# Two decoder layers on one core: pair-wide operations, f32 roots as split pairs, layer 1's low weight parts made ahead, and a searched order

## The chip, the cores and the metric

The kernel runs on one core of a Trainium2 chip. The time is device microseconds of one execution of the whole program; the median of several executions is compared. PE is the matmul engine, PEld its weight loads, DVE, ACT and POOL the vector, scalar and general engines, and SP the engine whose queue issues nearly all DMA transfers.

## The reference

Two layers over 1024 tokens of width 1024, all in float32. Each layer has one input projection feeding four mixers, a norm of each mixer's output, one output projection, and a gated FFN:

```python
for l in range(DEPTH):
    proj = rmsnorm(x, attn_norm[l]) @ w_in[l]
    (c_q, c_kv, k_r, g_b, g_c, u_conv, u_pool, q_sw, k_sw, v_sw) = jnp.split(proj, pts, axis=-1)
    y_a = mla_attention(c_q, c_kv, k_r, mla_q_norm[l], mla_kv_norm[l], w_uq[l], w_ukv[l], cos, sin)
    y_b = short_gated_conv(g_b, g_c, u_conv, conv_w[l])
    y_c = multiscale_pool(u_pool, pool_w[l], pool_scale[l])
    y_d = swa_sink_attention(q_sw, k_sw, v_sw, swa_sinks[l], slopes)
    gf = jnp.stack([y_a, y_b, y_c, y_d], axis=2)
    gf = gf * lax.rsqrt(jnp.mean(gf * gf, axis=-1, keepdims=True) + RMS_EPS)
    x = x + (gf.reshape(b, s, D_MIX) * mix_norm[l]) @ w_o[l]
    gate, up = jnp.split(rmsnorm(x, ffn_norm[l]) @ w_gate_up[l], 2, axis=-1)
    x = x + (jax.nn.silu(gate) * up) @ w_down[l]
return rmsnorm(x, final_norm)
```

`y_d` is attention in a window of 128 tokens with two key heads for four query heads; a sink logit per head is added to the softmax's denominator. The widths are 256 per mixer, 2816 in the FFN.

## The kernel before

**Precision.** Every operand of a matmul is held as two fp32r parts: a high part (an ACT cast, L342 or L216) and a low part (a DVE subtraction of the high part from the f32 value, L345 or L217). `split` does this for one tile, with an optional gain per row (L347 on ACT, L348 on DVE). `mm3` (L322) makes three matmuls of each term: high by high, high by low, low by high. The activations are transposed: 128 channels in the partitions, tokens along the row, in two halves of 512 tokens (`t` = 0, 1). SBUF is cut into 47 slots of 128 x 1024, each a pair of halves; `F.half`, `F.pair`, `R.half` and `R.pair` take them as f32 or fp32r.

**Stages of a layer.** (1) The mixers: 15 blocks of `w_in` (128 output channels each; 48 matmuls per block for both halves) with their consumers, then the latent attention with the output projection's blocks for groups b, c, d woven in, then the rest of the output projection. (2) The gate and up products, as a fast 2x2 algorithm with seven products instead of eight; `combine` (four calls) makes its sums of activations, `hb[N1]`, `hb[N2]`, `hb[T3]`, `hb[T4]`, out of half tiles. (3) The down projection with the same algorithm: 28 units (`units`, seven products by four blocks) of 33 matmuls each. Its weights come by `dn_raw` two units ahead and are split one unit ahead; its activations come back from DRAM (`ad`) by `dn_acts`.

**Weights.** `weights` loads a block as f32 (up to 512 KB), casts it on ACT and subtracts on DVE, into one of two ring places. `expect_layer` lists a layer's 15 `w_in` blocks and 8 `w_o` blocks in the order of use (the first three `w_in` blocks of layer 0 are loaded apart), `ahead` fetches the next one.

**Keys and queries of the window attention.** The key tile `pk` is scaled to f32 per half (L421). For each key head its 64 rows are cast and subtracted into their own rows of two tiles and again into the other 64 rows (L604 to L607), since a query tile holds its high part in one half of the rows and its low part in the other (`swa_q`, L529 to L534). `swa_unit` makes one block of 128 tokens for a key head: scores (L638), a biased minimum on DVE (L648), the exponent on ACT with its sum (L661), and the sink's exponent (DVE L671, ACT L672), which is added to the sum (L673).

**Roots.** `SumSq` adds up squares (ACT L377/L386, DVE L388/L394). `rnorm` sums over the partitions with a matmul by a matrix of ones and takes the inverse root by Ln, Exp and one correction (L411 to L417). If the object was made with `pair`, the sum is split into high and low first, and two fp32r matmuls with `ones_r` follow (L402); otherwise one f32 matmul with `ones` does it (L405), which the trace records as two. The entry norm, groups c and d and the query rank use L405.

**The order.** All instructions are traced once, and the class `Order` makes a list schedule from modelled costs: an order for each engine, a PSUM bank for each tile and a slot for each tile by its modelled end. `scheduled_kernel` repeats tracing and planning four times, keeps the plan with the shortest modelled span, and imposes its order on every engine's queue (SP's among them).

Of the kernel before, what the change touches and what calls it, by code (L numbers as in the profile page):

```python
# [13 lines left out]
F32 = mybir.dt.float32  # L14
# [5 lines left out]
P = 128  # L20
# [17 lines left out]
N_U = 47  # L38

# [83 lines left out]
def trunk_kernel(ctx: ExitStack, tc: tile.TileContext, ins, out, given=None, ends=None):  # L123
# [80 lines left out]
    def weights(src, n):  # L204
        if n > 2 * P:
            s = F.pair()
            raw = F.ap2(s)
            sp.dma_start(raw[:, :n], src)
            hi, lo = (R.ap2(i) for i in ring_next())
            F.free_pair(s)  # L210
        else:
            raw = wpool.tile([P, 2 * P], F32, name="vraw", tag="vraw")
            sp.dma_start(raw[:, :n], src)
            hi = wpool.tile([P, 2 * P], F32R, name="vhi", tag="vhi")
            lo = wpool.tile([P, 2 * P], F32R, name="vlo", tag="vlo")
        act.copy(hi[:, :n], raw[:, :n])  # L216
        dve.tensor_tensor(out=lo[:, :n], in0=raw[:, :n], in1=rd(hi[:, :n]), op=ALU.subtract)  # L217
        return hi, lo
# [16 lines left out]
    def expect(f, *args):  # L235
        stream.append((f, args))

    def expect_layer(l):
        for m in (2, 3, 0, 4, 5, 6, 1, 13, 14, 10, 11, 12, None, 7, 8, 9):
            if m is None:  # L240
                expect(rope_weights, l)
            else:
                if l or m not in (2, 3, 0):
                    expect(weights, ins["w_in"][l, m], 2 * HT)
        for d in range(NK):
            expect(weights, ins["w_o"][l, d, :, 2 * P :], 6 * P)
# [113 lines left out]
    class SumSq:  # L360
# [9 lines left out]
        def add(self, t, f, cols=whole, after=None):  # L370
            e = EPS * self.n / P
            m = self.done[t, cols.start] = self.done.get((t, cols.start), 0) + 1
            if self.acc[t] is None:
                self.acc[t] = F.half()
            a = F.ap(self.acc[t])[:, cols]
            if m == 1:
                sq = act.activation(a, f, AF.Square)  # L377
                if after is not None:
                    behind(sq, after)
                if self.n == P:  # L380
                    dve.tensor_scalar(out=a, in0=a, scalar1=e, scalar2=None, op0=ALU.add)
# [4 lines left out]
            act.activation(q, f, AF.Square)  # L386
            if m == self.n // P - self.held.get((t, cols.start), 0):
                dve.scalar_tensor_tensor(  # L388
                    out=a, in0=q, scalar=e, in1=a, op0=ALU.add, op1=ALU.add
                )  # L390
# [89 lines left out]
    for l in range(L):  # L480
# [34 lines left out]
        def ytiles(g):  # L515
            y[g] = [[F.half() for _ in range(2)] for _ in range(2)]
# [4 lines left out]
        def swa_q(m, pp):  # L521
            for t in range(2):
                f = tmp()
                dve.scalar_tensor_tensor(
                    out=f, in0=pp[t], scalar=0.125, in1=r_of(t), op0=ALU.mult, op1=ALU.mult
                )
                e, o = R.half(), R.half()
                qs[2 * m][t], qs[2 * m + 1][t] = e, o
                act.copy(R.ap(e)[hd], f[hd])  # L529
                act.copy(R.ap(o)[tl], f[tl])  # L530
                dve.tensor_tensor(
                    out=R.ap(e)[tl], in0=f[hd], in1=rd(R.ap(e)[hd]), op=ALU.subtract
                )
                dve.tensor_tensor(  # L534
                    out=R.ap(o)[hd], in0=f[tl], in1=rd(R.ap(o)[tl]), op=ALU.subtract
                )
# [61 lines left out]
        kk = [[R.pair(), R.pair()] for _ in range(2)]  # L598
        for t in range(2):
            f = tmp()  # L600
            mul_to(f, pk[t], r_of(t))
            for g, own, oth in ((0, hd, tl), (1, tl, hd)):
                k1, k2 = R.ap(kk[g][0] + t), R.ap(kk[g][1] + t)
                act.copy(k1[own], f[own])  # L604
                act.copy(k1[oth], f[own])
                dve.tensor_tensor(out=k2[own], in0=f[own], in1=rd(k1[own]), op=ALU.subtract)
                dve.tensor_tensor(out=k2[oth], in0=f[own], in1=rd(k1[own]), op=ALU.subtract)  # L607
# [19 lines left out]
        def swa_unit(g, i):  # L627
# [42 lines left out]
            sk = par[:, l * PC_N + PC_SINK + 2 * g : l * PC_N + PC_SINK + 2 * g + 2]  # L670
            dve.tensor_tensor(out=es, in0=nm, in1=sk, op=ALU.add)  # L671
            act.activation(es, es, AF.Exp)  # L672
# [79 lines left out]
        def group_split(g, t):  # L752
            for c in range(2):
                s = y[g][c][t]
                mixed[g, c, t] = half_split(F.ap(s), pcol(l, PC_MIX + 2 * "abcd".index(g) + c))
                F.free(s)
# [51 lines left out]
        for ct in range(2):  # L808
# [37 lines left out]
            F.free_pair(b)  # L846
            for t in range(2):
                h, lo = half_split(dst[:, t * HT : (t + 1) * HT])
# [10 lines left out]
        for t in HALVES:  # L859
            group_split("c", t)  # L860
# [7 lines left out]
        sq_q = SumSq(2 * P)  # L868
        for m in range(2):
            pp = project() if m else nextp  # L870
            for t in range(2):
                f = tmp()
                mul_to(f, pp[t], r_of(t))
                cq[m][t] = half_split(f, pcol(l, PC_QN + m))
                sq_q.add(t, f)
            swa_some(2)
# [306 lines left out]
        def combine(j):  # L1183
# [7 lines left out]
            n1, n2, t3, t4 = tmp("tp"), tmp("tp"), tmp("tp"), tmp("tp")  # L1191
# [7 lines left out]
            hb[T3][j] = half_split(t3)  # L1199
# [8 lines left out]
            hb[T4][j] = half_split(t4)  # L1208
# [27 lines left out]

        def pair_split(s, after=None):
            h, lo = R.pair(), R.pair()
            split(R.ap2(h), R.ap2(lo), F.ap2(s), after=after)
            return h, lo  # L1240
# [146 lines left out]
        for t in HALVES:  # L1387
            group_split("d", t)
# [3 lines left out]
        for n, (h, t) in enumerate(steps):  # L1392
# [8 lines left out]
            if n == 0:  # L1401
# [10 lines left out]
                group_split("b", 1)  # L1412
                group_split("b", 0)
# [369 lines left out]
        tail = []  # L1783
        for n, (c, m) in enumerate(units):
            if n + 2 < len(units):
                raws.append(dn_raw(*units[n + 2]))
# [67 lines left out]
class Order:  # L1854
# [10 lines left out]
    def __init__(self, traced, edges, banks=True):  # L1865
# [114 lines left out]
    def run(self, rank, back=False):  # L1980
# [5 lines left out]
        late, cost, kind = self.LATE[back], self.cost, self.kind  # L1986
        left = [len(w) for w in wait]
# [16 lines left out]
        for _ in range(self.n):  # L2004
            best = None
            for e in self.ENGINES:
                due(e, free[e])
                if not now[e] and not later[e]:
                    continue
                t = free[e] if now[e] else later[e][0][0]  # L2010
# [5 lines left out]
            due(e, t)  # L2016
            k = heapq.heappop(now[e])[1]
            seen, taken = cost[k]
            order[e].append(k)
# [17 lines left out]
            for j, sync in ahead[k]:  # L2037
# [9 lines left out]
                if not left[j]:  # L2047
                    heapq.heappush(later[self.engine[j]], (ready[j], j))
        return end, order

    def find(self, passes=3):
# [6 lines left out]
        return best  # L2058

# [38 lines left out]
def scheduled_kernel(fresh, ins_of, rounds=4):  # L2098
# [18 lines left out]
    plan = Order(traced, nc.dependency_edges)  # L2117
    end, best = plan.find()[2], None
    for _ in range(rounds):
        given = plan.banks(end), plan.ends(end, asked)  # L2120
        nc, traced, asked = trace(*given)
        plan = Order(traced, nc.dependency_edges)
        span, order, end = plan.find()
        if best is None or span < best[0]:
            best = span, given, order
# [134 lines left out]
```

## Time and profile before

| what | us |
|---|---|
| median of 3 runs | 2050.09 (2048.81 to 2051.84) |
| the profiled execution | 2051.07 |
| its span, first to last instruction | 2049.3 |
| PE busy | 2029.5 |
| DVE busy | 1521.4 |
| ACT busy | 988.8 |
| POOL busy | 568.7 |

Times in the trace count from the span's start. A group's row in a list by shape shows line, engine, operation, output from input, shapes and count, then busy us and the mean ns of one, then the engine's idle time before these instructions with what ended it. A timeline's row shows start us, length us and count of merged instructions; matmuls overlap in a pipeline and their ends are modelled, so the length of a merged row is the start of its last matmul plus one whole duration. A DMA row gives count, KB each and median us from issue to landing.

### The profile page before, as it was taken

To read this page: it belongs to the slowest core of one execution; us is meant where nothing else is said; L and a number is where in the kernel's file an instruction comes from. 1 tells how busy PE (TensorE), PEld (TensorE's weight loads), DVE (VectorE), ACT (ScalarE), POOL (GpSimd) and SP (SyncE) were. 2 spreads that over 40 slices of the span, in tenths; PEclk is the share of its full clock that TensorE was granted. 3 is DMA by queue.
4 is the path that set the end of the run, shared out by engine and by line. 5 is a ranking of instruction groups with operands and counts; after the bars stand their busy time and mean duration, and the time that the engine had idled before them with its cause. 6 is when DMAs were issued, how large, how long until landed. Compare 5 with 4: busy or idle time off the path is not lost.

```text
span 2049.3 us, 26536 instructions
## 1 busy us (share of the span) xinstructions
PE 2029.5 (99%) x9422; PEld 1675.6 (82%) x9422; DVE 1521.4 (74%) x2443; ACT 988.8 (48%) x1737; POOL 568.7 (28%) x428
## 2 busy tenths in 40 slices
PE   9999999999999999999999999999999999999998
PEld 7887888878888888888888878888788888888887
DVE  8779978997666768655657898889966666685555
ACT  7447657753333335434433666667433333354342
POOL 0100000047786772000001000000577777710000
PEclk9999999999999999999999999999999999999999
DMA  5431232334555556766424213232455555487552
GB/s 203 97 76 41 74 104 79 141 134 154 199 174 187 180 167 250 269 217 197 157 59 94 52 52 102 74 108 110 150 176 187 176 175 176 162 298 258 178 188 87
DMA packets 144294, 305.51 MB, mean 149 GB/s; under 512 B 13985, under 2 KB 61089, under 8 KB 144161
## 3 DMA queue, kind: packets, MB, share of 16 engines
q1 hardware_dynamic: 139680, 292.27, 41.8%
q0 software_dynamic: 4480, 11.54, 3.2%
q8 instruction: 74, 1.21, 0.2%
q14 instruction: 60, 0.48, 0.1%
HBM read 219.34 MB, written 94.90 MB: 153 GB/s over the span
## 4 chain that ended last, share of the span: by engine, by line
PE 91%; DVE 5%; issue 1%; DMA 1%; ACT 1%; POOL 0%; SPq 0%; DVEq 0%; ACTq 0%; POOLq 0%
PE ps_mm L322 35%; PE ps_s L322 28%; PE ps_t L322 10%; PE ps_pv L322 8%; PE ps_pv L1090 2%; PE ps_t L1078 1%; DVE u L345 1%; PE ps_s L1024 1%; PE ps_s L1026 1%; PE ps_s L1025 1%; DMA u<-in_w_gu 1%; PE ps_s L896 1%; DVE u L348 1%; PE ps_pv L699 1%; PE ps_s L638 1%
## 5 line engine op out<-in xcount | busy, mean ns | idle before, releaser
L322 PE MATMUL ps_mm<-u,u 128*128 128x512 f32 (+1 forms) x3378 | 833.3, 390 | 4.4 <-ACT u L342 1.5
L322 PEld LDWEIGHTS ps_mm<-u,u 128*128 128x128 f32 x3378 | 615.0, 188 | 131.3 <-issue 5.5
L322 PE MATMUL ps_s<-u,u 128*128 128x512 f32 x2670 | 634.4, 390 | 2.8 <-DVE u L345 1.7
L345 DVE TENSOR_TENSOR u<-u,u 128x1024 fp32r<-128x1024 f32 (+2 forms) x400 | 453.3, 1152 | 231.6 <-ACT u L342 161.1
L322 PEld LDWEIGHTS ps_s<-u,u 128*128 128x128 f32 x2670 | 500.4, 188 | 110.8 <-DVE u L345 4.0
L342 ACT CAST u<-u 128x1024 fp32r<-128x1024 f32 (+2 forms) x400 | 345.8, 882 | 456.2 <-PE ps_mm L322 72.1
L322 PE MATMUL ps_t<-u,u 128*128 128x512 f32 (+1 forms) x1124 | 254.2, 378 | 1.1 <-DVE u L1309 1.1
L322 PEld LDWEIGHTS ps_t<-u,u 128*128 128x128 f32 x1124 | 202.1, 188 | 41.7 <-DVE u L1309 1.6
L1502 POOL TENSOR_TENSOR tp<-tp,u 128x512 f32<-128x512 f32 x80 | 126.3, 1579 | 345.0 <-ACT tp L1500 345.0
L322 PE MATMUL ps_pv<-u,u 128*128 128x512 f32 x744 | 177.1, 389 | 0.0
L322 PEld LDWEIGHTS ps_pv<-u,u 128*128 128x128 f32 x744 | 139.6, 188 | 29.1
L296 POOL DMA_DIRECT2D gd<-in_w_gu x24 | 22.1, 921 | 421.5 <-PE ps_t L322 283.9
L1087 POOL MEMSET u<- 128x128 f32 x32 | 6.1, 221 | 431.3 <-PE ps_pv L1090 148.8
L1500 ACT ACTIVATE tp<-tp 128x512 f32<-128x512 f32 x80 | 50.6, 632 | 147.9 <-DVE tp L421 147.8
L347 ACT ACTIVATE u<-u,par 128x512 fp32r<-128x512 f32 x100 | 70.4, 717 | 37.4 <-DVE u L421 11.0
L342 ACT CAST u<-ps_t 128x512 fp32r<-128x512 f32 (+3 forms) x132 | 65.1, 503 | 47.9 <-PE ps_t L1078 26.7
L348 DVE SCALAR_TENSOR_TENSOR u<-u,par,u 128x512 fp32r<-128x512 f32 x100 | 73.3, 745 | 17.6 <-ACT u L347 17.4
L345 DVE TENSOR_TENSOR u<-ps_t,u 128x512 fp32r<-128x512 f32 (+3 forms) x132 | 75.4, 580 | 12.7 <-ACT u L342 10.9
L1580 POOL TENSOR_TENSOR u<-u,u 128x352 f32<-128x352 f32 x64 | 82.7, 1293 | 2.9 <-DMA u<-in_w_dn 1.5
L1580 POOL TENSOR_TENSOR u<-u 128x352 f32<-128x352 f32 x64 | 82.1, 1284 | 4.6 <-DMA u<-in_w_dn 3.9
L386 ACT ACTIVATE tn<-u 128x512 f32<-128x512 f32 (+1 forms) x91 | 52.9, 596 | 57.2 <-DVE u L1771 47.9
L1290 POOL TENSOR_TENSOR u<-u 128x512 f32<-128x512 f32 x38 | 69.5, 1829 | 21.8 <-DVE u L345 21.8
(203 smaller groups left out, 2347.4 us busy)
## 6 DMA issues: line engine op xcount, KB each, us to landing
u<-in_w_gu SPq DMA_DIRECT2D x84, 512.0 KB, 4.2
ad<-u SPq DMA_DIRECT2D x154, 256.0 KB, 2.4
u<-ad SPq DMA_DIRECT2D x70, 512.0 KB, 4.7
u<-in_w_dn SPq DMA_DIRECT2D x64, 352.0 KB, 3.6
qd<-u SPq DMA_DIRECT2D x64, 352.0 KB, 2.6
u<-qd SPq DMA_DIRECT2D x32, 512.0 KB, 5.0
u<-in_w_in SPq DMA_DIRECT2D x28, 512.0 KB, 3.5
u<-in_w_dn SPq DMA_DIRECT2D x24, 512.0 KB, 5.2
```

Of the source, the lines that this page charges most:

```text
L296: paced(pool.dma_start(d, a, **more))
L322: last_mm = pe.matmul(o, w, r, start=start and k == 0 and i == 0, stop=stop and k == n - 1 and i == 2, skip_group_check=again,)
L342: a = act.copy(hi, f)
L345: dve.tensor_tensor(out=lo, in0=f, in1=rd(hi), op=ALU.subtract)
L347: a = act.activation(hi, f, AF.Copy, scale=gain)
L348: dve.scalar_tensor_tensor(out=lo, in0=f, scalar=gain, in1=rd(hi), op0=ALU.mult, op1=ALU.subtract)
L386: act.activation(q, f, AF.Square)
L1090: pe.matmul(py[:, c0:], v_of(j, h), R.ap(s)[:, c0:], start=j == 0 and n == 0, stop=j == nj - 1 and n == 1,)
L1290: pool.tensor_tensor(out=q4, in0=q4, in1=F.ap(self.raw[1] + 1), op=ALU.add)
L1500: last_silu = act.activation(g, g, AF.Silu)
L1502: pool.tensor_tensor(out=g, in0=g, in1=r, op=ALU.mult)
L1580: pool.tensor_tensor(out=o, in0=a, in1=b, op=ALU.add)
```

## The change

Six edits, all in one step:

- **Low parts made ahead.** In layer 0's down projection (units 2 to 27), `prepare` loads each of layer 1's 23 weight blocks, splits it, and stores the low part to DRAM. In layer 1 `weights` loads raw values and the stored low part, and only casts the high part.
- **Roots.** `SumSq.add_pair` adds squares over both halves at once and, if `pair` is set, splits the sum. Groups c and d and the query rank are set to `pair`; the entry norm is not.
- **Halves joined.** Window queries and keys, `group_scale`, `group_split`, the pool's output, the query rank's split and the splits in `combine` work on 1024 columns where they worked on two tiles of 512.
- **Key copies.** The key tiles' other 64 rows are filled by four SP transfers a layer (256 KB each) instead of casts and subtractions.
- **Sink.** The sink's exponent takes the sink as its bias: two ACT instructions of one column a unit instead of a DVE addition and an ACT instruction of two columns.
- **Planner.** It plans twice (costs of DVE and ACT as modelled, and 3% longer), one round each instead of four. Each plan is improved by 30 random changes of the ranks where PE waits, kept if the modelled span doesn't grow; the order taken is the one with the smallest mean over six trials with random delays.

```diff
+SLOW = (1.0, 1.03)
+PREP = (1, 27)
...
+    def prepare(key, src, n):
+        s, h, lo = F.pair(), R.pair(), R.pair()
+        raw = F.ap2(s)[:, :n]
+        sp.dma_start(raw, src)
+        split(R.ap2(h)[:, :n], R.ap2(lo)[:, :n], raw)
+        F.free_pair(s)
+        R.free_pair(h)
+        prepared[key] = dpool.tile([P, n], F32, name="ph%s%d_%d" % key)
+        sp.dma_start(prepared[key], rd(R.ap2(lo)[:, :n]))
+        R.free_pair(lo)
+
-    def weights(src, n):
+    def weights(src, n, key=None):
...
+            if key in prepared:
+                sp.dma_start(rd(lo[:, :n]), prepared[key])
+                act.copy(hi[:, :n], raw[:, :n])
+                return hi, lo
...
+    def pair_split(s, gain=None, after=None):
+        h, lo = R.pair(), R.pair()
+        split(R.ap2(h), R.ap2(lo), F.ap2(s), gain, after)
+        return h, lo
...
+        def add_pair(self, f):
+            e = EPS * self.n / P
+            m = self.done[None] = self.done.get(None, 0) + 1
+            if m == 1:
+                a = F.pair()
+                self.acc = [a, a + 1]
+                act.activation(F.ap2(a), f, AF.Square)
+                return
+            a, q = self.acc[0], F.pair()
+            act.activation(F.ap2(q), f, AF.Square)
+            dve.scalar_tensor_tensor(
+                out=F.ap2(a), in0=F.ap2(q), scalar=e, in1=F.ap2(a), op0=ALU.add, op1=ALU.add
+            )
+            F.free_pair(q)
+            if self.pair:
+                h, lo = pair_split(a)
+                self.hl = {t: (h + t, lo + t) for t in range(2)}
...
         for t in range(2):
-            f = tmp()
-            mul_to(f, pk[t], r_of(t))
-            for g, own, oth in ((0, hd, tl), (1, tl, hd)):
-                k1, k2 = R.ap(kk[g][0] + t), R.ap(kk[g][1] + t)
-                act.copy(k1[own], f[own])
-                act.copy(k1[oth], f[own])
-                dve.tensor_tensor(out=k2[own], in0=f[own], in1=rd(k1[own]), op=ALU.subtract)
-                dve.tensor_tensor(out=k2[oth], in0=f[own], in1=rd(k1[own]), op=ALU.subtract)
+            mul_to(F.ap(fp + t), pk[t], r_of(t))
+        f = F.ap2(fp)
+        for g, own, oth in ((0, hd, tl), (1, tl, hd)):
+            k1, k2 = (R.ap2(i) for i in kk[g])
+            act.copy(k1[own], f[own])
+            dve.tensor_tensor(out=k2[own], in0=f[own], in1=rd(k1[own]), op=ALU.subtract)
+            for k in (k1, k2):
+                sp.dma_start(rd(k[oth]), rd(k[own]))
...
-            dve.tensor_tensor(out=es, in0=nm, in1=sk, op=ALU.add)
-            act.activation(es, es, AF.Exp)
+            for h in range(2):
+                act.activation(
+                    es[:, h : h + 1],
+                    nm[:, h : h + 1],
+                    AF.Exp,
+                    bias=pcol(l, PC_SINK + 2 * g + h),
+                    scale=1.0,
+                )
...
-            sg = SumSq(2 * P, g in "b")
+            sg = SumSq(2 * P, g in "bcd")
+            for c in range(2):
+                sg.add_pair(F.ap2(y[g][c][0]))
             for t in range(2):
-                for c in range(2):
-                    sg.add(t, F.ap(y[g][c][t]))
-                r = sg.rnorm(t)
-                for c in range(2):
-                    a = F.ap(y[g][c][t])
-                    mul_to(a, a, F.ap(r))
-                F.free(r)
+                sg.rnorm(t)
+            for c in range(2):
+                a = F.ap2(y[g][c][0])
+                mul_to(a, a, F.ap2(sg.acc[0]))
+            F.free_pair(sg.acc[0])
...
-        sq_q = SumSq(2 * P)
+        sq_q = SumSq(2 * P, True)
...
-            hb[N2][j] = half_split(n2)
-            hb[N1][j] = half_split(n1)
+            h, lo = pair_split(sn)
+            hb[N1][j], hb[N2][j] = (h, lo), (h + 1, lo + 1)
...
         for n, (c, m) in enumerate(units):
+            while not last and n > PREP[0] and len(todo) * (PREP[1] - PREP[0]) > 23 * (PREP[1] - n) and todo:
+                w, i = todo.popleft()
+                src = ins["w_in"][l + 1, i] if w == "in" else ins["w_o"][l + 1, i, :, 2 * P :]
+                prepare((w, l + 1, i), src, 2 * HT if w == "in" else 6 * P)
...
+    def trial(self, order):
+        ends = (self.run(None, fixed=order, draw=random.Random(n))[0] for n in range(6))
+        return sum(map(max, ends)) / 6
...
+        for _ in range(tries):
+            at = draw.choices([t for t, _ in found], [w for _, w in found])[0]
+            new = [
+                r + draw.gauss(0.0, 1) if at - 40 < t < at + 5 else r for r, t in zip(rank, end)
+            ]
+            e, o = self.run(new)
+            if max(e) <= span:
+                rank, span, order, end = new, max(e), o, e
+                found = self.waits(order, end)
```

More of the change, by code (lines that the diff above doesn't have):

```diff
@@ L2015, in run @@
             t, e = best
[L2016 to L2018 removed]
+            if fixed is not None:
+                k = fixed[e][len(order[e])]
+            else:
+                due(e, t)
+                k = heapq.heappop(now[e])[1]
+            seen, taken = cost[k]
+            if draw:
+                late = 2.5 * draw.random() if draw.random() < 0.25 else 0.0
+                if e in ("DVE", "Activation", "Pool"):
+                    more = draw.gauss(0.0, 0.02) * seen
+                    seen, taken = seen + more, taken + more
             order[e].append(k)
@@ L2116, in scheduled_kernel @@
     nc, traced, asked = trace(None, None)
[L2117 to L2125, printed above, removed]
+    first, tried, found = Order(traced, nc.dependency_edges), asked, []
+    for slow in SLOW:
+        plan, asked, first.slow = first, tried, slow
+        end = plan.find()[2]
+        for _ in range(rounds):
+            given = plan.banks(end), plan.ends(end, asked)
+            nc, traced, asked = trace(*given)
+            plan = Order(traced, nc.dependency_edges, slow)
+            best = plan.find()
+            end = best[2]
+            order = plan.improve(best, 30)[1]
+            found.append((plan.trial(order), given, order))
+    best = min(found, key=lambda x: x[0])
     return trace(*best[1], best[2])[0]
```

131 lines of the change are left out of this document (85 added, 46 removed).

## The prediction

> **What bounds the kernel now.** I read the page's first two parts first, then the busy time by stage, then the timeline of PE where it stalls. The page's rows say that PE is busy for 99% of the span.
>
> ```profile
> span 2049.3 us, 26536 instructions
> ...
> PE 2029.5 (99%) x9422; PEld 1675.6 (82%) x9422; DVE 1521.4 (74%) x2443; ACT 988.8 (48%) x1737; POOL 568.7 (28%) x428
> ...
> PE   9999999999999999999999999999999999999998
> PEld 7887888878888888888888878888788888888887
> DVE  8779978997666768655657898889966666685555
> ```
>
> The stages are cut at the entry (0 to 20 us), layer 0's mixers (20 to 450), its gate and up products (to 808), its down projection (to 1032), and the same three for layer 1. Each row has the stage's length, then busy us and instructions of PE, weight loads, DVE, ACT and POOL, the granted clock, the DMA share and GB/s.
>
> ```profile
> 0.00:20.00 20.00, 17.23 (x72) 13.04 (x73) 13.06 (x25) 14.55 (x24) 0.20 (x4) 1.00 0.89 313
> 20.00:450.00 430.00, 427.66 (x2069) 351.03 (x2068) 377.93 (x800) 268.63 (x565) 31.08 (x38) 1.00 0.31 93
> 450.00:808.00 358.00, 358.00 (x1577) 295.17 (x1576) 254.34 (x255) 128.95 (x177) 250.55 (x174) 1.00 0.54 182
> 808.00:1032.00 224.00, 224.00 (x990) 185.40 (x989) 139.22 (x169) 105.21 (x139) 1.81 (x1) 1.00 0.62 214
> 1032.00:1450.00 418.00, 412.96 (x2000) 338.26 (x1999) 346.21 (x753) 245.75 (x526) 20.24 (x32) 1.00 0.29 84
> 1450.00:1823.00 373.00, 373.00 (x1646) 308.46 (x1645) 261.13 (x269) 136.12 (x185) 263.04 (x180) 1.00 0.53 179
> 1823.00:2050.00 227.00, 216.66 (x1080) 184.26 (x1078) 129.47 (x177) 89.58 (x123) 1.81 (x1) 0.98 0.57 197
> ```
>
> Two readings matter. In the gate-up and down stages PE has no idle time at all, so nothing done there can help, only harm. In the two mixer stages DVE is busy 88% (377.93/430) and 83% (346.21/418) of the time, and PE shows 2.34 + 5.04 = 7.38 us of idle time. That is less than what is lost, because the modelled end of a matmul covers the start of a gap:
>
> ```profile
> 1425.50 2.88 PE L322 MATMUL ps_t<-u,u 128*128 128x512 f32 x12
> 1428.22 2.88 PE L322 MATMUL ps_pv<-u,u 128*128 128x512 f32 x12
> ...
> 1439.33 0.61 PE L322 MATMUL ps_pv<-u,u 128*128 128x512 f32 x2
> 1440.62 1.02 PE L322 MATMUL ps_mm<-u,u 128*128 128x512 f32 x3 [0.68 <-ACT u L342]
> 1442.14 2.31 PE L322 MATMUL ps_mm<-u,u 128*128 128x512 f32 x9 [0.49 <-DVE u L345]
> 1444.29 0.39 PE L322 MATMUL ps_s<-u,u 128*128 128x512 f32 x1
> ```
>
> Undisturbed, twelve 512-column matmuls take 1428.22 - 1425.50 = 2.72 us, 0.227 each. From 1439.33 to 1444.29 there are 14, worth 3.17 us, in 4.96 us: 1.79 us lost, of which 1.17 (0.68 + 0.49) is shown as idle. By this ratio, 1.53, my estimate of what PE loses in the two mixer stages is 7.38 x 1.53 = 11.3 us. What releases PE there are splits on ACT and DVE. So a gain can come from two places only: less PE work, and earlier DVE and ACT results in the mixer stages.
>
> **The roots.** The sum of squares of groups c and d and of the query rank goes through an f32 matmul with `ones` (L405). The change sends it as two fp32r halves through `ones_r` (L402), as group b does already.
>
> ```profile
> L405 PE MATMUL ps_t<-u,ones x28: 590/592/697, 20.5 to 1210.2; 128*128 128x512 f32 x28
> ```
>
> ```profile
> 1194.67 0.63 PE L913 MATMUL ps_t<-u,e_r 128*128 128x512 f32 x2
> 1195.18 1.13 PE L405 MATMUL ps_t<-u,ones 128*128 128x512 f32 x2
> 1195.74 2.18 PE L322 MATMUL ps_mm<-u,u 128*128 128x512 f32 x7
> 1197.76 1.02 PE L405 MATMUL ps_t<-u,ones 128*128 128x512 f32 x2
> 1198.22 1.03 PE L322 MATMUL ps_mm<-u,u 128*128 128x512 f32 x2
> ```
>
> ```profile
> 1415.40 0.62 PE L402 MATMUL ps_t<-u,ones_r 128*128 128x512 f32 x2
> ```
>
> 28 records at two per root are 14 roots: two at the entry, which stay, and two halves x three sums x two layers = 12, which change. The first root above starts at 1195.18, and the seven matmuls behind it end at 1195.74 + 2.18 = 1197.92. Taking off six intervals (1.36) and one whole matmul (0.39) leaves 0.99 us for the root. The second: 1198.22 + 1.03 - 1197.76 - 0.227 - 0.39 = 0.87. The fp32r pair of L402 costs two intervals, 0.45 us (its row, 0.62, is one interval and one whole matmul). A root thus saves 0.42 to 0.54 us, twelve save 5.0 to 6.5; I take **-5.5 us**. PE is the bound where they stand, so this arrives in full unless the extra split (below) makes PE wait.
>
> **DVE and ACT work.** Durations for both layers:
>
> ```profile
> L348 DVE SCALAR_TENSOR_TENSOR u<-u,par,u 128x512 fp32r<-128x512 f32 x100 | 73.3, 745 | 17.6 <-ACT u L347 17.4
> ...
> L345 DVE TENSOR_TENSOR u<-tp,u 128x512 fp32r<-128x512 f32 x32 | 23.2, 737 | 1.9 <-ACT u L342 1.9
> ...
> L388 DVE SCALAR_TENSOR_TENSOR u<-tn,u 128x512 f32<-128x512 f32 x29 | 19.9, 685 | 3.3 <-ACT tn L386 3.0
> ...
> L606 DVE TENSOR_TENSOR u<-te,u 64x512 fp32r<-64x512 f32 x8 | 5.5, 685 | 0.2
> ...
> L834 DVE SCALAR_TENSOR_TENSOR u<-u,cst,u 128x1024 f32<-128x1024 f32 x4 | 5.1, 1272 | 0.1
> ...
> L671 DVE TENSOR_TENSOR sm<-sm,par 128x2 f32<-128x2 f32 x32 | 4.9, 154 | 0.3
> ```
>
> and in layer 1's mixer stage (window 1032 to 1450):
>
> ```profile
> L217 DVE TENSOR_TENSOR u<-u,u 128x1024 fp32r<-128x1024 f32 x9 | 11.0, 1217 | 0.0
> ...
> L217 DVE TENSOR_TENSOR u<-u,u 128x768 fp32r<-128x768 f32 x8 | 7.6, 952 | 0.0
> ```
>
> DVE, for one layer, with 1.22 us for a joined subtract (L217's row) and 1.27 for a joined scaled one (L834's):
> - keys: 8 subtracts of 0.685 become 2 of 1.22, the other rows' copies going to four SP transfers: -3.0
> - SWA queries: 8 of 0.685 become 4 of 1.22: -0.6
> - `combine`: 16 of 0.737 become 8 of 1.22: -2.0
> - scaled splits of groups b, c, d and the query rank: 16 of 0.745 become 8 of 1.27: -1.8
> - additions of squares (8 of 0.685 become 4 of 1.27) and scalings by the root (12, also at 0.685, become 6 of 1.22): -1.3
> - three new splits of the sums: +3.7
> - the sink sums (L671) leave, 16 of 0.154: -2.5.
>
> That is -7.5 us a layer. In layer 1 the subtracts of the prepared weights leave too, 11.0 + 7.6 = 18.6 us within this stage (the other six come before it), so 26 of its 346 us, 8%. ACT loses as many copies as it gains and is far from full (245.75 of 418).
>
> None of it is on PE's path by itself: it counts only where DVE's queue makes PE wait, in the 11.3 us above. With 2% less DVE work in layer 0, 8% less in layer 1 and an order searched against PE's waits, I take half of them as recovered, **-6 us**. The ends: nothing at all or everything (-11). On the other side, a joined operation gives its first half later: where a 512-wide subtract took 0.74, the first half now waits 1.22 plus the second half's producer (0.69). The list above joins some 24 places a layer; if a fifth of the 48 let PE wait 1 us, that is the bound of a loss, **+10**.
>
> **Key copies.** The last key subtract of layer 0 ends at 44.98, and the first score matmul (L638) starts at 52.6, so 7.6 us are free.
>
> ```profile
> 44.29 0.69 DVE L607 TENSOR_TENSOR u<-te,u 64x512 fp32r<-64x512 f32 x1
> ```
>
> ```profile
> L638 PE MATMUL ps_s<-u,u x128: 220/281/385, 52.6 to 1159.5; 128*128 128x256 f32 x112, 128*128 128x128 f32 x16
> ```
>
> ```profile
> u<-u SPq DMA_DIRECT2D x8, 128.0 KB, 2.2
> ```
>
> A transfer of half the size takes 2.2 us (the key rope copies). The four here (256 KB each) overlap, and only the second's end is needed for the first head pair: between 2.2 and 4.4 us, inside the 7.6. Price **0**; if the cover is gone, up to four in a row, 8.8 - 7.6 = 1.2 us. By the Trainium skill (SBUF — State Buffer, Door 1: The DMA port swizzle), 64 partitions reach only half of the ports, 196 GB/s instead of 328 measured at 1 MiB; an estimate by that is 4 x 256 KB / 196 = 5.4 us for all four, which the gap still covers. No run here has shown that rate.
>
> **Weights made ahead.** During layer 0's down projection 23 weights (15 of 512 KB, 8 of 384) are loaded, split and their low parts stored: 23 casts, 23 subtracts, 46 transfers with 11.0 MB in each direction. DVE there has 224 - 139 = 85 us free for the 26 needed, ACT 119 for 23. The DMA engines are the question:
>
> ```profile
> DMA packets 16389, 41.82 MB, mean 209 GB/s; under 512 B 1822, under 2 KB 5022, under 8 KB 16377
> ```
>
> ```profile
> 800.00:850.00 50.00, 50.00 (x222) 41.39 (x221) 40.09 (x47) 29.76 (x37) 3.62 (x2) 1.00 0.93 333
> ```
>
> The first row is 820 to 1020 us. With 22.0 MB more it carries 63.8 MB in 200 us, 319 GB/s; the second shows 333 GB/s at a share of 0.93, and PE not idle. So it fits, at about nine tenths, and the weights are fetched two units (15 us) before use, three times a transfer's usual 4 to 5 us. Price **0**; the loss, if it doesn't fit, is the slower rival. SP issues 46 more transfers; the stores wait for a subtract, and raw weights and activations queue behind them, with the same 15 us of lead. In layer 1 each low part is a second load of 512 KB beside the first, at a DMA share of 0.29: covered by the 10.9 us that PE needs for a projection (48 matmuls).
>
> **Sum**, against the profiled execution's own 2051.07 us (span 2049.3 and 1.8 around it): 2051.07 - 5.5 - 6.0 = 2039.6. That execution is 0.98 us above the median of the runs, 2050.09, so the forecast is **2039 us**, 0.5% faster.
>
> **Rivals.**
> 1. Only the roots pay: DVE's relief goes into idle time, since PE waits for chains of operations and not for DVE's total. For it: PE's waits are few and short. Time: 2050.09 - 5.5 = 2044.6.
> 2. The searched order closes most of the gaps: 2050.09 - 5.5 - 11.3 = 2033, and some us lower if the hidden part is larger than my ratio says. For it: DVE is at 83 to 88%, and every wait is for DVE or ACT. Against: the search works on costs that the chip need not follow.
> 3. Slower: the down projection of layer 0 is short of DMA. If reads and writes together carry only 265 GB/s (between its 214 now and the 333 of its fullest part), 63.8 MB need 241 us instead of 200; less the 15 us of lead and the stretch from 1020 to 1032 this leaves about 14 us of PE waiting: 2050 - 5.5 + 14 = 2058. It decides from about 280 GB/s downwards (228 us, against 200 + 15 + 12). For it: 0.93 at the stage's start already; against: PE ran through that stretch. By the Trainium skill (DMA: Bandwidth & Descriptors, Specifications) a core gets some 358 GB/s of HBM; by that figure the 319 would fit.
> 4. The joined halves and the new splits make PE wait where it didn't: half of the bound, +5, cancels the roots: about 2050.
>
> **How the numbers follow.** Forecast 0.50 (own range 2034 to 2046), rival 1 0.14, rival 2 0.12, rival 3 0.15, rival 4 0.09. What a measurement of this kernel can tell from no change is 0.2%, 4.1 us, so faster means below 2046.0. Forecast, rival 2 and three quarters of rival 1 are faster: 0.73. Same: the rest of rival 1 and most of rival 4, 0.11. Slower: rival 3 and a little of 4, 0.16. The range 2029 to 2054 leaves out most of rival 3 and the edge of rival 2.
>
> **What would show it.** Roots: L405 falls from x28 to x4 in the profile, L402 rises by 24. Stalls: PE's idle time in the two mixer stages falls from 7.4 to 3 or 4 us, and DVE's busy time by 7 and 26 us. Rival 3: the down stage of layer 0 is longer than 224 us, with PE waiting for casts that wait for `ad` or `qd` loads at a DMA share near 1. Rival 4: new PE waits for L345 or L348 of 1024 elements. The forecast is wrong if the mixer stages don't shorten by more than the 5.5 us of the roots, or if a stage that had no idle time gets some.

## The result, and the profile after

| | median us | range |
|---|---|---|
| before, 6 runs | 2049.69 | 2048.71 to 2051.84 |
| after, 6 runs | 2042.56 | 2041.44 to 2043.14 |

The ratio is 0.9964, 95% interval 0.9951 to 0.9976: 7.1 us less. The profiled executions went from 2051.07 to 2043.14, 7.9 us less. The page of the changed kernel:

```profile
span 2041.4 us, 26572 instructions
...
PE 2025.0 (99%) x9422; PEld 1676.2 (82%) x9422; DVE 1534.3 (75%) x2339; ACT 1011.0 (50%) x1724; POOL 577.5 (28%) x428
```

ACT is 22 us busier than before (988.8), about what the 23 extra casts take. DVE is 13 us busier than before (1521.4) although it runs 104 instructions fewer (the 23 subtracts only move from layer 1 to layer 0). Some unchanged instructions of the two gate-up stages take longer: those of L421 on `tp` tiles, L467 now, went from 922 to 988 ns on average. The planner alone (e2 below) shows the same, 976 ns and 1533.8 us in all; why was not examined. The same stretches of time as in the prediction (length; busy us and count of PE, weight loads, DVE, ACT, POOL; clock; DMA share; GB/s):

```profile
20.00:450.00 430.00, 428.90 (x2082) 352.86 (x2081) 377.13 (x747) 268.75 (x547) 32.55 (x40) 1.00 0.33 97
450.00:808.00 358.00, 357.51 (x1575) 295.01 (x1573) 256.66 (x256) 130.44 (x177) 253.44 (x172) 1.00 0.54 184
808.00:1032.00 224.00, 223.70 (x986) 185.23 (x987) 154.36 (x185) 123.79 (x158) 1.49 (x1) 1.00 0.89 322
1032.00:1450.00 418.00, 415.26 (x2026) 343.41 (x2025) 330.13 (x691) 250.23 (x516) 28.19 (x35) 1.00 0.36 105
1450.00:1823.00 373.00, 371.95 (x1640) 307.41 (x1639) 278.76 (x269) 138.84 (x188) 261.61 (x178) 1.00 0.56 188
```

The reader sees three things. PE's idle time in the mixer stages fell from 7.4 us to 1.10 + 2.74 = 3.8. The first down projection's DMA share rose from 0.62 to 0.89 and PE is idle for 0.3 us there. And the gate-up stages, which had no idle time, now have 0.5 and 1.05 us, at their ends.

Stages begin earlier in the changed kernel, so a fixed stretch holds a little more of the next stage. A cleaner measure is the start of the matmul of the same number (all kernels here have 9422 matmul records, numbered from 0, and nearly all stand within their stages). This table is worked out from the traces, in us from the span's start. Number 2139 is about the end of layer 0's mixers, 3717 the end of its gate-up stage, and 3899 lies in its down projection. 5276 lies inside layer 1's mixers, where each kernel has its own order, so it compares little; 6700 is their end, 8463 lies in the second down projection, 9421 is the last:

```
matmul no.   before    after    planner   planner   bank
                                alone     + roots   margin
 2139         450.2    446.5     446.4     450.0     446.6
 3717         808.9    804.9     805.1     809.0     804.7
 3899         850.1    847.2     846.3     850.3     845.9
 5276        1150.2   1148.7    1145.2    1149.1    1144.6
 6700        1450.1   1441.2    1438.2    1445.4    1437.3
 8463        1850.1   1842.5    1838.8    1845.3    1839.2
 9421        2039.9   2032.3    2028.6    2035.2    2029.0
```

After against before: 3.7 us gained by the end of layer 0's mixers, 1.0 us lost on entering the down projection (from 3.9 ahead to 2.9; the differences are taken before rounding), 6.0 us gained in layer 1 up to its gate-up stage (8.9 ahead), 1.3 us lost on entering the second down projection (7.6 ahead), nothing elsewhere. The other columns are experiments below.

**The roots** cost PE what was expected:

```profile
L451 PE MATMUL ps_t<-u,ones x4: 590/592/595, 19.9 to 37.2; 128*128 128x512 f32 x4
```

```profile
L448 PE MATMUL ps_t<-u,ones_r x52: 389/392/496, 145.3 to 1410.5; 128*128 128x512 f32 x52
```

Four f32 records are left (28 before), and 24 more split records (28 before). An f32 root took 0.87 us before: the median, over the twelve, of the time from its start to the start of the second matmul behind it, less one interval of 0.227 for the matmul between. Twelve take 10.4, and the 24 that took their place 5.4 at one interval each. That is 5.0 us less PE work. The Trainium skill (FP8 and Floating Point Precision, TensorE Precision Notes) says that a true FP32 product takes four passes through the array; 0.87 / 0.227 = 3.8 agrees.

**The losses at the entries.** Timeline of PE, DVE and ACT of the changed kernel at the second one:

```profile
1814.14 2.88 PE L343 MATMUL ps_s<-u,u 128*128 128x512 f32 x12
1818.06 2.11 PE L343 MATMUL ps_s<-u,u 128*128 128x512 f32 x8 [1.04 <-DVE tp L1775]
```

```profile
1816.18 1.23 DVE L366 TENSOR_TENSOR u<-u,u 128x1024 fp32r<-128x1024 f32 x1 [2.77 <-ACT u L363]
1817.33 0.68 DVE L1775 TENSOR_TENSOR tp<-ps_mm,tn 128x512 f32<-128x512 f32 x1
```

```profile
1815.10 1.05 ACT L363 CAST u<-u 128x1024 fp32r<-128x1024 f32 x1 [2.41 <-DMA u<-in_w_dn]
```

Read from below: a load of down weights lands late, so ACT's cast starts late, so DVE stands 2.77 us before the subtract, and behind it in the queue waits L1775, which reads the gate-up stage's last PSUM tile but one. The last product is the twelve matmuls from 1814.14, so the down projection could start at 1814.14 + 12 x 0.227 = 1816.86. The plan gave that tile's bank to its first unit, so PE waits for L1775, which ends at 1818.0. In the kernel before PE runs through both entries. At the second, its last product starts at 1823.08 and the down projection at 1825.80, and DVE reads that tile (L1718 there) in time:

```profile
1820.36 2.88 PE L322 MATMUL ps_mm<-u,u 128*128 128x512 f32 x12
1823.08 12.18 PE L322 MATMUL ps_s<-u,u 128*128 128x512 f32 x53
```

```profile
1823.65 0.68 DVE L1718 TENSOR_TENSOR tp<-ps_mm,tn 128x512 f32<-128x512 f32 x1
```

**A loss in layer 1**, PE and ACT of the changed kernel:

```profile
1101.86 0.39 PE L343 MATMUL ps_mm<-u,u 128*128 128x512 f32 x1
1103.67 0.39 PE L755 MATMUL ps_pv<-u,u 128*128 128x256 f32 x1 [1.42 <-ACT u L363]
```

```profile
1102.09 1.04 ACT L230 CAST u<-u 128x1024 fp32r<-128x1024 f32 x1 [1.76 <-DMA u<-in_w_in]
1103.04 0.58 ACT L363 CAST u<-ps_t 128x512 fp32r<-128x512 f32 x1
```

The same pattern: a weight's cast (L230) waits for its load, and a cast that PE needs stands behind it.

### The profile page after: what moved, and what is told of

Read it like the earlier page. It is cut to its first block, busy times and chain, and to the rows that moved or that the text cites. A ratio compares the mean times of both kernels' runs of the same rounds, so it can differ in the third digit from the quotient of the medians.

```text
span 2041.4 us, 26572 instructions
## 1 busy us (share of the span) xinstructions
PE 2025.0 (99%) x9422; PEld 1676.2 (82%) x9422; DVE 1534.3 (75%) x2339; ACT 1011.0 (50%) x1724; POOL 577.5 (28%) x428
## 3 DMA queue, kind: packets, MB, share of 16 engines
q8 instruction: 74, 1.21, 0.2%
## 4 chain that ended last, share of the span: by engine, by line
PE 94%; DVE 3%; DMA 1%; ACT 1%; issue 0%; SPq 0%; DVEq 0%; ACTq 0%
PE ps_mm L343 36%; PE ps_s L343 29%; PE ps_t L343 12%; PE ps_pv L343 8%; PE ps_pv L1151 2%; PE ps_t L1139 1%; PE ps_s L1085 1%; PE ps_s L1086 1%; PE ps_s L1087 1%; PE ps_s L957 1%; PE ps_pv L755 1%; PE ps_s L689 1%; PE ps_t L743 1%; PE ps_t L448 1%; DMA u<-in_xT 1%; DVE u L369 0%
## 5 line engine op out<-in xcount | busy, mean ns | idle before, releaser
L366 DVE TENSOR_TENSOR u<-u,u 128x1024 fp32r<-128x1024 f32 (+3 forms) x439 | 514.3, 1195 | 181.0 <-ACT u L363 123.2
L363 ACT CAST u<-u 128x1024 fp32r<-128x1024 f32 (+3 forms) x439 | 387.6, 904 | 386.6 <-DMA u<-ad 57.8
L343 PE MATMUL ps_t<-u,u 128*128 128x512 f32 (+1 forms) x1138 | 259.6, 378 | 0.1
L368 ACT ACTIVATE u<-u,par 128x512 fp32r<-128x512 f32 (+1 forms) x92 | 71.8, 792 | 36.4 <-DVE u L467 11.6
L1637 POOL TENSOR_TENSOR u<-u 128x352 f32<-128x352 f32 x64 | 77.9, 1217 | 21.5 <-DMA u<-in_w_dn 20.8
L1349 POOL TENSOR_TENSOR u<-u 128x512 f32<-128x512 f32 x38 | 74.5, 1959 | 19.8 <-DVE u L366 16.2
L369 DVE SCALAR_TENSOR_TENSOR u<-u,par,u 128x512 fp32r<-128x512 f32 (+1 forms) x92 | 76.0, 839 | 5.3 <-ACT u L368 5.2
L467 DVE TENSOR_TENSOR tp<-tp,u 128x512 f32<-128x512 f32 x76 | 75.1, 988 | 2.1
```

The lines of the kernel that those rows point to most:

```text
L343: last_mm = pe.matmul(o, w, r, start=start and k == 0 and i == 0, stop=stop and k == n - 1 and i == 2, skip_group_check=again,)
L363: a = act.copy(hi, f)
L366: dve.tensor_tensor(out=lo, in0=f, in1=rd(hi), op=ALU.subtract)
L368: a = act.activation(hi, f, AF.Copy, scale=gain)
L369: dve.scalar_tensor_tensor(out=lo, in0=f, scalar=gain, in1=rd(hi), op0=ALU.mult, op1=ALU.subtract)
L467: dve.tensor_tensor(out=o, in0=a, in1=b, op=ALU.mult)
```

## The experiments

Theory A, which the prediction held: the roots' PE time and DVE's relief in the body of the kernel bring the gain. Rival B: the searched order closes the gaps, whatever the body does. Every variant is planned anew, so its order differs too. Three seeds of the new planner, on the same work, span 2.5 us (e2, e9, e10); where a variant was run in one order alone, a difference of that size shows little. The old planner draws no random numbers, so nothing bounds this for e1 and e3. Each ratio is against runs of the kernel before in the same set.

| run | us | before | ratio (95%) |
|---|---|---|---|
| e1 body, old planner | 2045.83 | 2049.71 | 0.9983 (0.9974 to 0.9992) |
| e2 planner alone | 2039.99 | 2049.71 | 0.9953 (0.9939 to 0.9967) |
| e9 planner alone, seed 2 | 2041.02 | 2049.70 | 0.9956 (0.9943 to 0.9970) |
| e10 planner alone, seed 3 | 2042.48 | 2049.70 | 0.9964 (0.9952 to 0.9977) |
| e4 whole change, seed 2 | 2041.22 | 2049.71 | 0.9957 (0.9944 to 0.9969) |
| e3 roots alone, old planner | 2052.97 | 2049.71 | 1.0014 (1.0005 to 1.0023) |
| e5 planner and roots | 2046.58 | 2050.74 | 0.9980 (0.9971 to 0.9989) |
| e7 change, f32 roots | 2046.39 | 2050.74 | 0.9978 (0.9970 to 0.9987) |
| e6 change, nothing made ahead | 2048.33 | 2050.74 | 0.9987 (0.9978 to 0.9996) |
| e12 planner and made ahead | 2041.57 | 2049.56 | 0.9963 (0.9949 to 0.9977) |
| e8 change, low parts stored twice | 2041.65 | 2050.74 | 0.9956 (0.9943 to 0.9968) |
| e11 change, bank margin | 2039.37 | 2049.70 | 0.9948 (0.9936 to 0.9961) |

### e1: the body without the planner

The changed `trunk_kernel` with the class `Order` and `scheduled_kernel` of before.

> All edits of the change but its planner: the order comes from the planner of before (four rounds, shortest modelled span). Theory A (the body pays: roots 5.5 us, DVE relief some 2 us, and the planner brings little): 2040 to 2044 us, against 2049.7 before and 2042.6 with the whole change; the two gaps at the entry to the down projection (1.0 and 1.3 us) may go. Rival B (the searched order closes the gaps of the mixer stages, the body brings the roots alone): 2044 to 2047 us, with PE idle in the mixer stages of 6 to 8 us as before.

2045.83 us: 3.9 us less than before. That is no more than the roots' 5.0, so in this order the DVE relief showed no gain. It lies in B's span and outside A's, and its time fits rival 1 of the prediction (only the roots pay). But PE's idle time in the mixer stages fell to 1.56 + 3.20 = 4.8 us, where B had it stay at 6 to 8:

```profile
20.00:450.00 430.00, 428.44 (x2077) 351.75 (x2076) 375.68 (x747) 267.56 (x546) 32.92 (x39) 1.00 0.32 96
...
1032.00:1450.00 418.00, 414.80 (x2018) 341.10 (x2017) 328.57 (x689) 248.15 (x514) 23.85 (x34) 1.00 0.35 105
```

And e3 below shows the roots alone losing time under this planner, so the 3.9 us can't simply be booked as theirs.

### e2, e9, e10: the planner without the body

The old `trunk_kernel` with the changed planner, with

```diff
-        draw = random.Random(1)
+        draw = random.Random(2)
```

and 3 in e9 and e10.

> The kernel before with the changed planner only: same instructions, another order. Theory A: 2047 to 2051 us. Rival B: 2043 to 2046 us, PE idle in the mixer stages halved from 7.4 us.

> The kernel before with the changed planner only, random seed 2. If 2040.0 us with seed 1 was the planner's usual result: 2038 to 2042 us again, so the edits of the body bring nothing on top of the planner. If it was luck: 2043 us or more.

> The same with seed 3; the three seeds together bound what the random search does to the time of the unchanged work. Usual result: 2038 to 2042 us; luck: 2043 us or more.

2040.0, 2041.0 and 2042.5: on average 8.5 us less than before, with the instructions of before. The first lies below both theories' spans, and of the other two only the third is above the 2038 to 2042 that were given for a usual result. The page and the stretches of e2:

```profile
span 2038.0 us, 26549 instructions
...
PE 2024.8 (99%) x9422; PEld 1675.7 (82%) x9422; DVE 1533.8 (75%) x2443; ACT 989.4 (49%) x1737; POOL 562.4 (28%) x428
```

```profile
20.00:450.00 430.00, 428.79 (x2077) 352.74 (x2077) 378.53 (x800) 268.04 (x565) 33.52 (x40) 1.00 0.31 95
...
808.00:1032.00 224.00, 224.00 (x989) 185.42 (x988) 136.64 (x168) 103.29 (x137) 1.55 (x1) 1.00 0.61 206
1032.00:1450.00 418.00, 417.45 (x2036) 345.32 (x2035) 353.54 (x761) 249.07 (x531) 27.10 (x36) 1.00 0.29 86
```

PE's idle time in the mixer stages is 1.21 + 0.55 = 1.8 us, less than in the changed kernel, while DVE is as busy as before (353.54 against 346.21; between the same matmuls, from the start of layer 1 to number 6700, 343.3 against 346.0). So DVE's total was not what made PE wait. Which part of the new planner brings this (the two sets of costs, the single round, the random changes or the trials with delays) was not run apart. The table of matmuls shows the same: e2 is 3 us ahead of the changed kernel at the 6700th, though its f32 roots cost 5.0 us more.

### e4: another seed for the whole change

> The changed kernel with another random seed in its search (2 for 1): the same work in another order. If the order is a matter of luck of a few us: between 2039 and 2046 us, with the 1 us gaps at other places (the entry to the down projection may have none). If the search always ends near the same order: 2042.6 within 1 us, with the same two gaps at the entry to the down projection.

2041.2 us. The gap at the first entry shrank to 0.2 us, the second stayed at 1.1 (PE's waits for L1775). The change with two seeds gave 2042.6 and 2041.2, the planner alone 2040.0 to 2042.5: no difference between them can be told. No order without the body has such a gap (before, e2, e9, e10, and e3, e5, e12 below). Of the six orders with the body and the old choice of bank five have one (e1, the change, e4, e6, e8), and e7 has none; whether the body leads the planner there or chance does was not tried.

### e3, e5, e7: the roots

e3 is the kernel before, e5 the kernel of e2, both with

```diff
-            sg = SumSq(2 * P, g in "b")
+            sg = SumSq(2 * P, g in "bcd")
...
-        sq_q = SumSq(2 * P)
+        sq_q = SumSq(2 * P, True)
```

and e7 is the changed kernel with these two lines put back.

> The kernel before with groups c and d and the query rank made as split pairs (twelve f32 root matmuls become 24 fp32r ones), half by half as group b was, old planner. If a root saves 0.46 us of PE and nothing else moves: 2049.7 - 5.5 = 2044.2 us. If the added splits (12 casts and 12 subtracts of 512 columns on DVE and ACT, 8.2 us of DVE in all) make PE wait instead: 2047 us or more.

> The kernel before with the changed planner and with groups c and d and the query rank as split pairs, half by half; halves not joined, no prepared weights, key copies and sink as before. If a root saves its PE time (0.87 us for an f32 root, 0.45 for the pair, twelve of them: 5.0 us) also under the new order: 2040.0 - 5.0 = 2035 us. If the added splits give it back as PE waits, as the run with the roots alone under the old planner suggests: 2039 to 2042 us.

> The changed kernel with the sums of groups c and d and of the query rank not split: their roots are f32 matmuls again, all else joined as in the change. If the pair saves 5.0 us net: 2042.5 + 5 = 2047.5 us. If the split's time on ACT and DVE (3 casts and 3 subtracts of 1024 columns a layer ahead of the root) gives it back: 2041 to 2044 us.

Without the other edits, the roots lose: 3.3 us slower than before under the old planner, and 4.2 us faster than before where the planner alone had 8.5. The second, 2046.6 us, is slower than either span that was expected of it. PE and ACT of e5 at its longest gap:

```profile
1188.54 0.74 PE L915 MATMUL ps_t<-u,e_r 128*128 128x512 f32 x2 [0.30 <-DVE tn L416]
1192.13 0.73 PE L324 MATMUL ps_mm<-u,u 128*128 128x512 f32 x2 [2.86 <-ACT u L218]
```

```profile
1188.67 0.63 ACT L414 ACTIVATE tn<-tn 128x512 f32<-128x512 f32 x1
1189.21 0.60 ACT L344 CAST u<-te 128x512 fp32r<-128x512 f32 x1
1189.77 0.63 ACT L415 ACTIVATE tn<-tn 128x512 f32<-128x512 f32 x1
1190.43 0.58 ACT L344 CAST u<-ps_t 64x512 fp32r<-64x512 f32 x1
1191.03 1.04 ACT L218 CAST u<-u 128x1024 fp32r<-128x1024 f32 x1
```

PE stands 2.86 us until the next weights are cast (L218), and that cast stands at the end of a full ACT queue of root and split work. e3 has a gap at the same place (2.3 us for the same cast, L216 there). In the changed kernel, with halves joined and layer 1's low parts made ahead, taking the split away seems to cost time: e7 is 0.9978 against 0.9964, 0.14% or 2.9 us, of the 5.0 that PE saves, and between its two expected times. The intervals overlap and each side is one order, so this much is not shown.

### e6, e12: the weights made ahead

e6 is the changed kernel with an empty list of weights to prepare:

```diff
-        todo = deque() if last else deque([...])
+        todo = deque()
```

e12 is the kernel of e2 with `prepare`, its use in `weights` and the loop that calls it.

> The changed kernel without the low parts made ahead: layer 1's weights are split in layer 1 as before. If DVE relief in layer 1 pays (the prediction's view): 2045 us or more, with layer 1's mixer stage 3 us longer. If making them ahead costs more than it brings: 2040 us or less. If it is hidden both ways: 2042 within 1.5 us. The DMA share of the first down projection falls from 0.89 to about 0.6.

> The kernel before with the changed planner and the low parts made ahead; roots, halves, key copies and sink as before. The three seeds of the planner alone gave 2040.0, 2041.0 and 2042.5 us (mean 2041.2), the whole change 2042.6. If making ahead saves about 5 us by itself, as its removal from the changed kernel suggests: 2036 us, the fastest of all. If it only pays for what the other edits add to ACT and DVE: 2040 to 2042 us.

Taken from the change it costs 0.9987 against 0.9964, 0.23% or 4.7 us, of which 3.3 lie between matmuls 3899 and 6700; by this number alone the relief of DVE in layer 1 pays. But added to the planner alone it brings nothing: 8.0 us less than before, inside the three seeds' 7.2 to 9.7. DVE is relieved there, from 343.3 to 328.8 us between the same matmuls of layer 1's mixers, and these take 410.3 us against 409.8 in e2:

```profile
1032.00:1450.00 418.00, 417.51 (x2034) 345.17 (x2033) 337.67 (x744) 249.48 (x531) 27.21 (x36) 1.00 0.36 104
```

So if it pays, it pays for what the other edits load onto ACT and DVE; e6 is one order, and its 4.7 us are less than twice the spread of the seeds. e6 shows such a load, on PE, DVE and ACT:

```profile
1247.50 0.29 PE L1087 MATMUL ps_s<-u,u 128*128 128x256 f32 x1
1249.11 0.73 PE L343 MATMUL ps_mm<-u,u 128*128 128x512 f32 x2 [1.32 <-ACT u L368]
1250.91 0.39 PE L1085 MATMUL ps_s<-u,u 128*128 128x256 f32 x1 [1.07 <-ACT u L1104]
```

```profile
1246.65 2.35 DVE L467 TENSOR_TENSOR u<-u,u 128x1024 f32<-128x1024 f32 x2
```

```profile
1247.90 2.29 ACT L368 ACTIVATE u<-u,par 128x1024 fp32r<-128x1024 f32 x2 [0.83 <-DVE u L467]
1250.10 0.67 ACT L1104 ACTIVATE u<-ps_s,sm 128x512 f32<-128x512 f32 x1
```

Two joined scalings hold DVE for 2.35 us, then two joined splits hold ACT for 2.29; PE waits 1.32 us for the first of these and then 1.07 for a softmax exponent queued behind the second. This is the loss that rival 4 of the prediction named, though PE waits for ACT here and not for DVE. It shows in e6; the changed kernel has no PE wait of this kind over 0.5 us.

### e8: twice the stores

```diff
         sp.dma_start(prepared[key], rd(R.ap2(lo)[:, :n]))
+        again = dpool.tile([P, n], F32, name="pz%s%d_%d" % key)
+        sp.dma_start(again, rd(R.ap2(lo)[:, :n]))
```

> The changed kernel with each low part stored twice, the second copy unused: 11 MB more written in the first down projection, 75 MB in 200 us or 375 GB/s by the count. If the DMA engines there still have room or the lead of the loads covers it: 2042 to 2044 us. If they were at their limit (0.89 busy at 322 GB/s): PE waits there for splits of late loads, 2048 us or more.

2041.65 us, no loss. Its first down projection:

```profile
808.00:1032.00 224.00, 223.23 (x984) 184.85 (x985) 154.88 (x186) 124.74 (x158) 1.49 (x1) 1.00 0.96 371
...
820.00:1020.00 200.00, 200.00 (x884) 165.61 (x883) 137.40 (x164) 108.52 (x140) 0.00 (x0) 1.00 0.99 381
```

The DMA engines moved 371 GB/s at a share of 0.96, and the 0.77 us that PE is idle there belong to the gap at the entry, before the transfers in question. From 820 to 1020 us alone they moved 381 GB/s at a share of 0.99, with PE busy all the time. Rival 3 falls: neither 322 nor 371 GB/s starved PE. Both figures of e8 lie above the 358 GB/s that the Trainium skill (DMA: Bandwidth & Descriptors, Specifications) gives as the HBM limit of a core, a stack's 716 divided by two cores. This program uses one core, and here the measurement decides.

### e11: a margin for the banks

In the planner's choice of a bank:

```diff
-            b = max(range(8), key=lambda b: free[b] if free[b] <= start else -free[b])
+            b = max(range(8), key=lambda b: free[b] if free[b] <= start - 1.5 else -free[b])
```

> The changed kernel whose planner takes a PSUM bank as free only 1.5 us after its modelled end. If the two gaps at the entry to the down projection (1.0 and 1.3 us) come from a bank that was to be freed just in time: both go, and the time is 2040 us or a little less. If only the order on DVE makes them: they stay, 2042 us.

2039.37 us, 10.3 less than before and 0.16% less than the change by the ratios, about as fast as the best order of the planner alone (2039.99, overlapping intervals). PE at the first entry and at two waits in the second gate-up stage:

```profile
804.43 7.87 PE L343 MATMUL ps_s<-u,u 128*128 128x512 f32 x34
...
1527.92 3.04 PE L343 MATMUL ps_s<-u,u 128*128 128x512 f32 x12 [0.68 <-DVE tp L1775]
1531.48 2.81 PE L343 MATMUL ps_t<-u,u 128*128 128x512 f32 x11 [0.53 <-DVE u L1551]
```

34 matmuls run through the entry without a gap. So do those of the second entry, although DVE stands almost as long there as in the changed kernel:

```profile
1812.18 9.68 PE L343 MATMUL ps_s<-u,u 128*128 128x512 f32 x42
```

```profile
1813.82 1.23 DVE L366 TENSOR_TENSOR u<-u,u 128x1024 fp32r<-128x1024 f32 x1 [2.57 <-ACT u L363]
1814.96 0.68 DVE L1775 TENSOR_TENSOR tp<-ps_mm,tn 128x512 f32<-128x512 f32 x1
```

DVE again stands 2.57 us for the late cast, and reads the last tile but one from 1814.96 to 1815.64. The down projection starts at 1812.18 + 12 x 0.227 = 1814.90, without waiting for it. So the gap came from the choice of bank, not from DVE's order alone. The two new gaps in the gate-up stage take 1.2 us of the gain back. One order shows it; other seeds, and the margin with the planner alone, were not run.

## Why the prediction was right, and where its steps were not

- **Time and direction**: 2039 was forecast, 2042.6 measured, within the range; faster, as given 0.73. The number owes something to luck: the planner alone gains 8.5, and the body, whose roots were to bring 5.5 of the 11.5, shows no gain on top of it.
- **Roots, -5.5 us**: PE's work fell by 5.0. That it "arrives in full unless the extra split makes PE wait" named the condition that decided: without the other edits the split made PE wait for more than it saved (e3, e5). With them perhaps 2.9 us arrive (e7 against the change), which is not clear of noise.
- **Stalls, -6 us**: the size was near up to the entries and the cause was wrong. Counting starts of matmuls, 3.9 us were gained up to the first entry and 6.0 in layer 1 up to the second, 4.9 beyond the roots' 5.0; the entries lost 2.3, which leaves 7.6 - 5.0 = 2.6. Idle time in the mixer stages fell to 3.8 us, as the prediction said (3 or 4). The step that failed is the one that put DVE's relief and the search together as one cause: the old planner with the whole body gained no more than the roots (e1), the new planner with nothing of the body gained 8.5 (e2, e9, e10). Rival 2 (the order closes most gaps) was the better description, but of the planner alone, and its 8.5 is short of the 11.3. On top of it the body's edits took back what they gave.
- **Joined halves, bound +10**: the loss is possible. e6 shows PE waiting 2.4 us behind joined operations; the changed kernel doesn't show it. What the joins cost by themselves was not run apart from the key copies and the sink, so their share stays open.
- **DVE's relief of 26 us in layer 1**: DVE's busy time in that stretch of time fell by 16, and between the same matmuls by 21 (346.0 to 325.2); in layer 0 by 4 (378.0 to 374.1), where 7.5 were put. Under the new planner such relief was no gain for PE (e12 against e2).
- **Made ahead, price 0**: right for the down projection (319 GB/s at nine tenths foreseen from 820 to 1020 us, 327 at 0.91 measured), and e8 showed room beyond it. In layer 1 a late weight load still held up a cast and with it PE by 1.42 us; e12 has the same second loads, and PE is idle there for 0.5 us in all, so they need not cost anything.
- **Key copies, price 0**: each transfer took 3.9 us in the median where 2.2 to 4.4 was put, and the first scores start at 53.6 instead of 52.6; no wait of PE points to them.
- **Not foreseen**: 2.3 us at the entries to the down projections. The prediction said of stages without idle time that a change could only harm them, and named idle time in such a stage as a sign of being wrong. That sign came, 0.5 and 1.05 us at the ends of the gate-up stages; the harm was sought in DMA, and it lay in the bank.

## What to carry to other kernels

In this kernel the bound engine waited in many short pieces, and the order of the other engines' queues decided, not their totals. Where that is so, reorder first, and test every saving again under the new order, since removing work may then show nothing. A joined operation is shorter than its two halves (1.22 us on DVE against twice 0.69) and delays whatever stands behind it in its queue. A plan that hands a buffer on just in time can turn a late transfer into a wait; in the one order that was tried, some slack cost less than it saved. And before a few us are credited to an edit, run the same work in several orders: here they alone span 2.5 us.

## What the runs showed of the hardware that was not expected

One core's transfers reached 371 GB/s on average over 224 us (e8), and 381 over 200 us at a DMA share of 0.99, without PE waiting for a weight meanwhile. And a busy PE hid more loss than its idle time showed: the planner alone took 11.3 us off the span (2049.3 to 2038.0), of which only 6.5 came from idle time (19.8 to 13.2 by span less busy time); the rest must lie under the modelled ends of the matmuls, since the work is the same, as the prediction's ratio of 1.53 said in kind (11.3 / 6.5 = 1.7).
